# The gate matrix of an expert layer by accumulating scatters instead of one-hot matrix products

## The chip, the cores and the metric

One core of one Trainium2 chip runs the kernel. The metric is the time of one execution on the device in microseconds (us). Before the change it is 2658.03 us, the median of 3 runs (2650.47 to 2663.66).

## The reference

The reference is one encoder layer on two sequences, a long one of 512 tokens and a short one of 256: attention of two kinds, gates, projections, and then a layer of experts. All is in float32. The change concerns the experts:

```python
q = (t @ w_query).reshape(T, PEER_HEADS, 2, PEER_HALF)
s1 = jnp.einsum('thc,hkc->thk', q[:, :, 0], sub_keys_1)
s2 = jnp.einsum('thc,hkc->thk', q[:, :, 1], sub_keys_2)
v1, i1 = lax.top_k(s1, PEER_TOPK)
v2, i2 = lax.top_k(s2, PEER_TOPK)
cand = (v1[..., :, None] + v2[..., None, :]).reshape(T, PEER_HEADS, PEER_TOPK * PEER_TOPK)
top, ci = lax.top_k(cand, PEER_TOPK)
e1 = jnp.take_along_axis(i1, ci // PEER_TOPK, axis=-1)
e2 = jnp.take_along_axis(i2, ci % PEER_TOPK, axis=-1)
idx = (e1 * PEER_KEYS + e2).reshape(T, PEER_HEADS * PEER_TOPK)
g = jax.nn.softmax(top, axis=-1).reshape(T, PEER_HEADS * PEER_TOPK)
u = expert_u[idx]
a = jax.nn.gelu(jnp.einsum('ted,td->te', u, t), approximate=False)
out = jnp.einsum('te,ted->td', g * a, expert_v[idx])
```

Each token picks 16 of 16384 experts in each of 8 heads, 128 in all, each with a gate g. The tables expert_u and expert_v hold 16384 rows of 1024 numbers, 64 MB each.

## The kernel before, in words

The front (function front, first for the short sequence "p", then for the long one "s") does attention, projections and norms. It ends with w_query in four chunks of two heads; the scores of each chunk go through top16 on VectorE.

The experts are done in two ways. The short sequence gathers (gather, L814): for each of its two tiles of 128 tokens, 128 indirect DMAs fetch one row of u per token into a tile gr (512 KB, three buffers), VectorE multiplies and sums it (L828), and later 128 more fetch rows of v that VectorE adds up (L836). These 512 gathers are issued by GpSimd (L821) and are spread over everything that follows, by fill, which emits a step of the one generator for so much of the other.

The long sequence is dense: all 16384 experts are computed for all 512 tokens, and a matrix of gates, zero nearly everywhere, picks. It runs in blocks of 128 experts. A u block (stage1, L733) loads 512 KB, splits them into a high and a low part (split, L139: ScalarE rounds, VectorE subtracts) and makes 24 products of 128x512 (mm3, L144) into pu; ScalarE applies Gelu to it. 28 of the 128 results go to DRAM (ad), the others stay in SBUF. A v block (stage2 in dense, L757) multiplies a block's activations with its gates gt, splits the product and 128 rows of v, and makes 24 products into eight outputs of 128x512. Five of them (held) stay in PSUM; the other three are summed over groups of four blocks and then added on VectorE (L807), since the u blocks that run beside them need banks too.

The gate matrix is built in between. pick (L635), once for each tile of 128 tokens with its 8 heads, chooses the top 16 sums and their experts; the products pr of 1600 elements run on GpSimd (L675). gbuild (L705) then makes, for every token, two one-hot matrices (o1 on VectorE, o2 shared by GpSimd, ScalarE and VectorE by the table BY) and multiplies them on TensorE (L724) into a 128x128 matrix of gates, which ScalarE evicts and a DMA writes to gd:

```python
eng.tensor_scalar(o2, iota, sl[t][1][:, tk:tk + 1], sl[t][2][:, tk:tk + 1], op0=ALU.is_equal, op1=ALU.mult)
pe.matmul(p[:, j * 128:(j + 1) * 128], lhsT=o1[:, q % 8 + j, :], rhs=o2, start=True, stop=True)
```

The generators fix the order in which instructions are emitted, and a scheduler then orders each engine's queue by its own estimate of times. On the chip every engine and every DMA queue runs its list in order.

Of the kernel before, what the change touches and what calls it, by code (L numbers as in the profile page):

```python
# [11 lines left out]
F32 = mybir.dt.float32  # L12
# [15 lines left out]
GCH = 32  # L28
# [4 lines left out]
FILL = (2.25, 0.0, 3.7)  # L33
FG = 2.25
FL = {"p": 1, "s": 3}
BY = "aavvvvppavvvvppp"
B1, B2, B3 = 3, 8, 6
AT, SU, GP = (0.45, 0.25, 0.5)
UE = 3
# [5 lines left out]
ORDER, SLB = ('pppbpbbb', 3)  # L45
U0, UP, UB = (10, 0.25, 0.08)
# [3 lines left out]
def tile_peer(ctx: ExitStack, tc: tile.TileContext, a: dict):  # L50
# [23 lines left out]
    iota = cp.tile([128, 128], F32, name="iota")  # L74
# [7 lines left out]
    def consts():  # L82
        """rope tables with the gains of the first 16 dims, gain columns"""
# [19 lines left out]
        nc.sync.dma_start(iota, a["iota"])  # L103
# [11 lines left out]
    sl, slp = {}, []  # L115
# [6 lines left out]
    gd = dr.tile([S_S // GCH, 128, 128, GCH], F32, name="gd")  # L122

    anchor, banchor, turn, tog = [None], [None], [0], [0]
# [68 lines left out]
    def proj(pool, src, kts, Th, Tl, nt, name, onpool=0, unit=1.0):  # L193
        """per token tile PSUM [128, 512] of T^T @ src"""
# [10 lines left out]
    def proj_halves(last, src, Th, Tl, nt, name, onpool, done, unit):  # L205
        """proj of 8 row blocks, the first half of the token tiles before the second, done(t, acc) after each half"""
# [87 lines left out]
    def along(gen, other, rate=1.0):  # L294
        """gen with rate steps of other after each of its own, then what is left of other"""
# [35 lines left out]
    def front(seq):  # L331
# [6 lines left out]
        with ExitStack() as fs:  # L338
# [23 lines left out]
            with tc.tile_pool(name="att" + seq, bufs=1, reuse_waits="tile") as ap_:  # L362
# [12 lines left out]
                def post(c, raws):  # L375
                    """norm, rope and transposes of the query and key heads of chunk c"""
# [58 lines left out]
                # blocks: qa 0..3, qb0 4..5, kb0 6..7, qb1 qb2 8..11, kb1 kb2 12..15, ka 16  # L435
# [4 lines left out]
                def soft_pv(sm, n, negm, den, out, kvs):  # L440
                    """exp of -sm[:, :n] + negm, denominators, transposes, PV into out"""
# [62 lines left out]
                    # the dilated patterns stay within a tile of the order by class; the maximum goes on from the first pattern's  # L504
# [82 lines left out]
            vv = [pk.tile([128, 16, 16], F32, tag=f"vv{t}", name="vv") for t in range(nt)]  # L587
            iu = [pk.tile([128, 16, 16], U32, tag=f"iu{t}", name="iu") for t in range(nt)]
            for c in range(4):
                acc = [ps_mm(f"pq{m}", m // 2) for m in range(4)]  # L590
                # the first chunk of the long sequence takes the first half of its tokens before the second
# [12 lines left out]
                for m in range(4):  # L604
                    hh = 4 * c + m
# [7 lines left out]
                    for t in range(nt):  # L613
                        top16(pp, ss[:, t, :], 128, vv[t][:, hh, :], iu[t][:, hh, :])
# [12 lines left out]
    def gates(pool, w):  # L627
        """softmax over the 16 of a head, from the scores less their maximum"""
        ac.activation(w, w, AF.Exp)
        sm = pool.tile([128, 8], F32, tag="gsm", name="gsm", bufs=1)  # L630
        ve.tensor_reduce(sm, w, op=ALU.add, axis=AX.X)
        ve.reciprocal(sm, sm)
        ve.tensor_tensor(w, w, sm.unsqueeze(2).broadcast_to([128, 8, 16]), op=ALU.mult)

    def pick(pool, seq, t, vv, iu):  # L635
        """top 16 of the sums, their experts and gates"""
        fi = pool.tile([128, 8, 2, 16], F32, tag="fi", name="fi", bufs=1)
        ac.copy(fi.rearrange("p h z k -> p (h z) k"), iu)
        v4 = vv.rearrange("p (h z) k -> p h z k", z=2)
        cand = pool.tile([128, 8, NCAND], F32, tag="cand", name="cand", bufs=1)  # L640
        pos = 0
        for i, n in enumerate(CAND[:8]):
            ve.tensor_tensor(cand[:, :, pos:pos + n], v4[:, :, 1, 0:n], v4[:, :, 0, i:i + 1].broadcast_to([128, 8, n]), op=ALU.add)
            pos += n
        ve.tensor_tensor(cand[:, :, pos:pos + 8], v4[:, :, 0, 8:16], v4[:, :, 1, 0:1].broadcast_to([128, 8, 8]), op=ALU.add)
        tv = pool.tile([128, 8, 16], F32, tag="tv", name="tv", bufs=1)
        ti = pool.tile([128, 8, 16], U32, tag="ti", name="ti", bufs=1)
        # experts of all candidates, then those at the chosen positions
        ce = pool.tile([128, 8, NCAND], F32, tag="ce", name="ce", bufs=1)
        i1 = pool.tile([128, 8, 16], F32, tag="i1", name="i1", bufs=1)  # L650
        ac.mul(i1, fi[:, :, 0, :], 128.0)
        pos = 0
        for i, n in enumerate(CAND[:8]):
            gp.tensor_tensor(ce[:, :, pos:pos + n], fi[:, :, 1, 0:n], i1[:, :, i:i + 1].broadcast_to([128, 8, n]), op=ALU.add)
            pos += n
        gp.tensor_tensor(ce[:, :, pos:pos + 8], i1[:, :, 8:16], fi[:, :, 1, 0:1].broadcast_to([128, 8, 8]), op=ALU.add)
        yield 1
        for h in range(8):
# [3 lines left out]
        tf = pool.tile([128, 8, 16], BF16, tag="tf", name="tf", bufs=1)  # L662
        ve.tensor_copy(tf, ti)
        e = []
        for z in range(2):
            ez = pool.tile([128, 8, 16], F32, tag=f"e{z}", name=f"e{z}", bufs=1)
            e.append(ez)
        ex = pool.tile([128, 8, 16], F32, tag="ex", name="ex", bufs=1)
        yield 2
        for h in range(0, 8, 2):  # L670
            eq = pool.tile([128, 2, NCAND, 16], BF16, tag="eq", name="eq", bufs=2 if seq == "s" else 1)
            pr = pool.tile([128, 2, NCAND, 16], F32, tag="pr", name="pr", bufs=2 if seq == "s" else 1)
            ve.tensor_tensor(eq, posx.unsqueeze(1).broadcast_to([128, 2, NCAND, 16]),
                             tf[:, h:h + 2, :].unsqueeze(2).broadcast_to([128, 2, NCAND, 16]), op=ALU.is_equal)
            gp.tensor_tensor(pr, eq, ce[:, h:h + 2, :].unsqueeze(3).broadcast_to([128, 2, NCAND, 16]), op=ALU.mult)  # L675
            ve.tensor_reduce(ex[:, h:h + 2, :], pr.rearrange("p h c s -> p h s c"), op=ALU.add, axis=AX.X)  # L676
            yield 2
        if seq == "p":
            ve.tensor_tensor(pw[t].rearrange("p (h s) -> p h s", s=16), tv, tv[:, :, 0:1].broadcast_to([128, 8, 16]), op=ALU.subtract)
            ve.tensor_copy(pidx[t], ex.rearrange("p h s -> p (h s)"))  # L680
            yield 2
            return
        wt = pool.tile([128, 8, 16], F32, tag="wt", name="wt", bufs=1)
        ve.tensor_tensor(wt, tv, tv[:, :, 0:1].broadcast_to([128, 8, 16]), op=ALU.subtract)
        gates(pool, wt)
        ei = pool.tile([128, 128], I32, tag="ei", name="ei", bufs=1)
# [296 lines left out]
```

## Time and profile before

| what | value |
|---|---|
| median of 3 runs | 2658.03 us (2650.47 to 2663.66) |
| profiled execution, span | 2664.0 us; its slowest run is 2663.66 us, so the span is the whole time |
| TensorE, VectorE, ScalarE, GpSimd busy | 2416.8, 1955.7, 992.3, 1084.5 us |
| moved by DMA | 590.52 MB, 222 GB/s in the mean |
| gathers (queue of GpSimd) | 512, 268.47 MB |

Busy times are unions of an engine's instructions; products on TensorE overlap, so their mean length (0.39 us) is longer than their spacing. The clock that TensorE was granted is 0.96 of full speed in the mean.

### The profile page before, as it was taken

What the parts mean: (1) busy time and instruction counts of PE and PEld (TensorE: products, weight loads), DVE (VectorE), ACT (ScalarE), POOL (GpSimd) and SP (SyncE); (2) the same over time, 40 slices, a digit from 0 to 9 for tenths busy, and PEclk for the clock granted to TensorE, in tenths of its full rate; (3) what the DMA queues carried; (4) which work ended last, traced back from release to release, by engine and by line L of the source; (5) the groups of instructions that cost most, each with busy time, mean ns of one, the idle gap of its engine ahead of it and who ended that gap; (6) DMA issues with size and microseconds to landing.
All of it is one profiled execution on the core that took longest, in us unless ns stands there. A gap on an engine that the chain in (4) does not pass through costs nothing.

```text
span 2664.0 us, 33871 instructions
## 1 busy us (share of the span) xinstructions
PE 2416.8 (91%) x11926; PEld 1993.4 (75%) x11926; DVE 1955.7 (73%) x4018; ACT 992.3 (37%) x1656; POOL 1084.5 (41%) x808
## 2 busy tenths in 40 slices
PE   8999989999989988887999998988889999999998
PEld 6787867768768767776777876777777777777776
DVE  6755798677698899667477777676667677676776
ACT  5764434443433334879322221222122222222221
POOL 0001241454554165879232444444334444444342
PEclk9999989999989999999999999999999999999999
DMA  6425433576984232534889887788778788787776
GB/s 210 133 88 167 143 99 114 181 228 213 316 277 145 90 103 102 198 147 174 307 298 316 290 284 271 265 278 280 258 254 285 268 283 276 258 273 269 263 248 214
DMA packets 250058, 590.52 MB, mean 222 GB/s; under 512 B 19488, under 2 KB 107296, under 8 KB 247840
## 3 DMA queue, kind: packets, MB, share of 16 engines
q1 hardware_dynamic: 169824, 278.99, 32.0%
q0 software_dynamic: 73728, 268.47, 29.1%
q10 hardware_dynamic: 6336, 40.90, 3.8%
q8 instruction: 94, 1.54, 0.2%
q14 instruction: 76, 0.62, 0.1%
HBM read 535.57 MB, written 51.38 MB: 220 GB/s over the span
## 4 chain that ended last, share of the span: by engine, by line
DMA 30%; DVE 21%; PE 21%; issue 15%; POOL 10%; ACT 3%; SPq 1%; DVEq 0%; POOLq 0%; ACTq 0%
DMA gr<-v,pidx 13%; DMA gr<-u,pidx 7%; POOL o2g L723 5%; POOL gr L821 4%; DMA vr<-v 4%; DVE x L836 3%; DVE gr L828 2%; DVE ex L676 2%; DMA wraw<-w_in 2%; DVE ul L141 2%; DVE vl L141 2%; DMA gl<-ad 2%; DVE wlo L141 1%; PE p_g L724 1%; PE pu L147 1%
## 5 line engine op out<-in xcount | busy, mean ns | idle before, releaser
L821 POOL DMA_INDIRECT gr<-v,pidx x256 | 346.7, 1354 | 490.6 <-DVE x L836 293.6
L821 POOL DMA_INDIRECT gr<-u,pidx x256 | 315.9, 1234 | 519.6 <-DVE gr L828 243.6
L836 DVE SCALAR_TENSOR_TENSOR x<-gr,act,x 128x1024 f32<-128x1024 f32 x256 | 328.5, 1283 | 208.7 <-DMA gr<-v,pidx 206.6
L828 DVE SCALAR_TENSOR_TENSOR gr<-gr,tok 128x1024 f32<-128x1024 f32 x256 | 337.4, 1327 | 180.6 <-DMA gr<-u,pidx 179.7
L145 PE MATMUL pu<-tTh,uh 128*128 128x512 f32 x1024 | 405.5, 396 | 26.3 <-ACT ga__15105 L745 5.9
L147 PE MATMUL pu<-tTh,ul 128*128 128x512 f32 x1024 | 406.5, 397 | 25.0 <-DVE ul L141 24.9
L146 PE MATMUL pu<-tTl,uh 128*128 128x512 f32 x1024 | 403.4, 394 | 0.0
L141 POOL TENSOR_TENSOR wlo<-wraw,whi 128x1024 fp32r<-128x1024 f32 x51 | 124.2, 2435 | 372.9 <-ACT whi L140 350.8
L140 ACT CAST uh<-ur 128x1024 fp32r<-128x1024 f32 x128 | 134.6, 1052 | 327.8 <-PE pu L146 238.0
L147 PEld LDWEIGHTS pu<-tTh,ul 128*128 128x128 f32 x1024 | 195.5, 191 | 71.1 <-DVE ul L141 30.6
L145 PEld LDWEIGHTS pu<-tTh,uh 128*128 128x128 f32 x1024 | 195.7, 191 | 69.8 <-ACT ga__15105 L745 6.4
L146 PE MATMUL held<-vl,ph 128*128 128x512 f32 x640 | 242.0, 392 | 0.0
L147 PE MATMUL held<-vh,pl 128*128 128x512 f32 x640 | 241.0, 390 | 0.0
L145 PE MATMUL held<-vh,ph 128*128 128x512 f32 x640 | 240.6, 396 | 0.0
L140 ACT CAST vh<-vr 128x1024 fp32r<-128x1024 f32 x128 | 134.3, 1049 | 278.4 <-DMA vr<-v 269.5
L145 PE MATMUL py<-vh,ph 128*128 128x512 f32 x384 | 166.2, 433 | 77.0 <-DVE y L807 63.2
L146 PEld LDWEIGHTS pu<-tTl,uh 128*128 128x128 f32 x1024 | 195.1, 190 | 40.7
L723 POOL TENSOR_SCALAR o2g<-iota,sl,sl 128x128 f32<-128x128 f32 x160 | 198.8, 1254 | 36.7 <-PE p_g L724 36.7
L140 ACT CAST whi<-wraw 128x1024 fp32r<-128x1024 f32 x137 | 143.7, 1049 | 159.7 <-DMA wraw<-w_in 53.7
L141 DVE TENSOR_TENSOR ul<-ur,uh 128x1024 fp32r<-128x1024 f32 x128 | 172.0, 1344 | 36.0 <-ACT uh L140 36.0
L141 DVE TENSOR_TENSOR vl<-vr,vh 128x1024 fp32r<-128x1024 f32 x128 | 156.4, 1222 | 21.4 <-ACT vh L140 21.2
L145 PEld LDWEIGHTS py<-vh,ph 128*128 128x128 f32 x384 | 78.3, 204 | 110.5 <-DVE y L807 77.2
(710 smaller groups left out, 5345.1 us busy)
## 6 DMA issues: line engine op xcount, KB each, us to landing
ur<-ublk SPq DMA_DIRECT2D x128, 512.0 KB, 4.7
vr<-v SPq DMA_DIRECT2D x128, 512.0 KB, 6.3
wraw<-w_in SPq DMA_DIRECT2D x80, 512.0 KB, 3.6
gd<-gs ACTq DMA_DIRECT2D x16, 2048.0 KB, 6.7
gt<-gd SPq DMA_DIRECT2D x32, 1024.0 KB, 10.1
wraw<-w_query SPq DMA_DIRECT2D x32, 512.0 KB, 3.8
wraw<-w_out SPq DMA_DIRECT2D x16, 512.0 KB, 4.1
gl<-ad SPq DMA_DIRECT2D x28, 256.0 KB, 7.1
```

What stands on the lines that cost most here:

```text
L140: i = ac.copy(hi, src)
L141: eng.tensor_tensor(lo, src, hi.bitcast(F32), op=ALU.subtract)
L145: pe.matmul(out, lhsT=lh, rhs=rh, start=first, stop=False)
L146: pe.matmul(out, lhsT=lh, rhs=rl, start=False, stop=False)
L147: pe.matmul(out, lhsT=ll, rhs=rh, start=False, stop=last)
L676: ve.tensor_reduce(ex[:, h:h + 2, :], pr.rearrange("p h c s -> p h s c"), op=ALU.add, axis=AX.X)
L723: eng.tensor_scalar(o2, iota, sl[t][1][:, tk:tk + 1], sl[t][2][:, tk:tk + 1], op0=ALU.is_equal, op1=ALU.mult)
L724: pe.matmul(p[:, j * 128:(j + 1) * 128], lhsT=o1[:, q % 8 + j, :], rhs=o2, start=True, stop=True)
L821: st = gp.indirect_dma_start(out=g, out_offset=None, in_=tab, in_offset=bass.IndirectOffsetOnAxis(ap=pidx[t][:, s:s + 1], axis=0))
L828: ve.scalar_tensor_tensor(g, g, 1.0, tok, op0=ALU.mult, op1=ALU.mult, accum_out=act[:, s:s + 1])
L836: ve.scalar_tensor_tensor(xt, g, act[:, s:s + 1], xt, op0=ALU.mult, op1=ALU.add)
```

## The change

Instead of one-hot matrices, the gates are added into a gate matrix in DRAM that was zeroed before (clear, in the front, by GpSimd's queue). For each of the four tiles t of 128 tokens there is one matrix gd[t]. A pick now covers one chunk of two heads for all tiles, so it has 32 experts per tile and token; scatter issues, for each of these 32 and each tile, one indirect DMA that adds 128 numbers (one per token) at 128 addresses. The products pr and the sums ce of pick move from GpSimd to VectorE. All u blocks come before the first v block, their activations all go through DRAM, and the v blocks then have all eight banks of PSUM. In this last part gathers have five more row buffers (gr2). The diff, cut to its core:

```diff
+U0, UP, US, GU = (8, 0.45, 0.16, 0.11)
+GV = 2.2
+GR2 = 5
-    gd = dr.tile([S_S // GCH, 128, 128, GCH], F32, name="gd")
+    gd = [dr.tile([128 * 128 * 128, 1], F32, name=f"gd{t}") for t in range(4)]
...
-            gp.tensor_tensor(pr, eq, ce[:, h:h + 2, :].unsqueeze(3).broadcast_to([128, 2, NCAND, 16]), op=ALU.mult)
-            ve.tensor_reduce(ex[:, h:h + 2, :], pr.rearrange("p h c s -> p h s c"), op=ALU.add, axis=AX.X)
+            ve.tensor_tensor(pr, eq.rearrange("p h c s -> p h s c"), ce[:, h:h + 2, :].unsqueeze(2).broadcast_to([128, 2, 16, NCAND]), op=ALU.mult)
+            ve.tensor_reduce(ex[:, h:h + 2, :], pr, op=ALU.add, axis=AX.X)
...
+        ve.tensor_scalar(si, ex.rearrange("p h s -> p (h s)"), 128.0, pcol, op0=ALU.mult, op1=ALU.add)
+        slots[c] = (si, wt.rearrange("p h s -> p (h s)"))
...
+    def scatter(c):
+        si, wt = slots[c]
+        for s in range(32):
+            for t in range(4):
+                k = t * 32 + s
+                gp.indirect_dma_start(out=gd[t], out_offset=bass.IndirectOffsetOnAxis(ap=si[:, k:k + 1], axis=0),
+                                      in_=wt[:, k:k + 1], in_offset=None, compute_op=ALU.add)
+            yield 1
+    def clear():
+        z = gpl.tile([128, D], F32, tag="gr", name="zero", bufs=3)
+        gp.memset(z, 0.0)
+        for t in range(4):
+            v = gd[t].rearrange("(p q k d) o -> q p k (d o)", p=128, q=4, d=D)
+            for q in range(4):
+                st = gp.dma_start(v[q], z.unsqueeze(1).broadcast_to([128, 4, D]))
...
-        if j < SP:
-            nc.scalar.dma_start(ad[j], ga)
-        else:
-            acts[j] = ga
+        nc.scalar.dma_start(ad[j], ga)
...
-        held = [psd.tile([128, 512], F32, name=f"held{i}") for i in range(5)]
+        held = [psd.tile([128, 512], F32, name=f"held{i}") for i in range(8)]
...
-                if own or g == ng - 1:
-                    ve.tensor_tensor(x[t][:, cs], py, x[t][:, cs], op=ALU.add)
+                mm3(held[i], ph[:, c], pl[:, c], vh[:, cs], vl[:, cs], j == 0, j == 127)
+                if j == 127:
+                    ve.tensor_tensor(x[t][:, cs], held[i], x[t][:, cs], op=ALU.add)
...
+            more = len(gp2) and s % (GR2 + 3) >= 3
+            g = (gp2[0] if more else pool).tile([128, D], F32, tag="gr2" if more else "gr", name="gr", bufs=GR2 if more else 3)
...
+    for c in range(4):
+        fill(pick(pks["s"][1], "s", c, *tops["s"][c]), ua, UP, due)
+    for c in range(4):
+        for _ in scatter(c):
+            due[0] += US * 4
+            gdue[0] += GU * 4
...
+    fill(dense(pv_, psd), gg, GV)
```

How the queues change is seen at three places. On GpSimd, the rows from the last products of the picks on stood like this (o2g is a one-hot matrix; a name in brackets is what the instruction waits for, DMASW being DMAs that GpSimd issued):

```order
L675 TENSOR_TENSOR pr<-eq,ce 128x1600 [waits DVE_49,Pool_49]
L675 TENSOR_TENSOR pr<-eq,ce 128x1600 [waits DVE_49]
L675 TENSOR_TENSOR pr<-eq,ce 128x1600 [waits DVE_49,Pool_49] x2
L723 TENSOR_SCALAR o2g<-iota,sl_9613,sl_9614 128x128 [waits PE_49] x27
L723 TENSOR_SCALAR o2g<-iota,sl_9910,sl_9911 128x128 [waits PE_49,Activation_49]
L723 TENSOR_SCALAR o2g<-iota,sl_9910,sl_9911 128x128 [waits PE_49] x39
```

and now, behind the last split of weights (gd_91 to gd_94 are the four matrices):

```order
L138 TENSOR_TENSOR wlo<-wraw,whi 128x1024 [waits DMAHW6_49,PE_49,Activation_49]
L696 DMA gd_91<-wt,si 2097152x1 [waits DMASW0_49,DVE_49]
L696 DMA gd_92<-wt,si 2097152x1 [waits DMASW1_49]
L696 DMA gd_93<-wt,si 2097152x1 [waits DMASW2_49]
L696 DMA gd_94<-wt,si 2097152x1 [waits DMASW3_49]
L696 DMA gd_91<-wt,si 2097152x1 [waits DMASW4_49,DMASW0_49]
L696 DMA gd_92<-wt,si 2097152x1 [waits DMASW5_49,DMASW1_49]
L696 DMA gd_93<-wt,si 2097152x1 [waits DMASW6_49,DMASW2_49]
L696 DMA gd_94<-wt,si 2097152x1 [waits DMASW7_49,DMASW3_49]
L696 DMA gd_91<-wt,si 2097152x1 [waits DMASW4_49]
```

In all, 512 scatters follow, 202 of them without a gather between, then 310 with 50 gathers; 104 gathers stand before them and 358 behind.

On SyncE, at the change from u to v blocks, the changed kernel has (ur is a u block, gt the gates, vr rows of v, gl activations):

```order
L716 DMA ur<-ublk 128x1024 [waits DMAHW6_49,DVE_49]
L737 DMA gt<-gd_91 128x512 [waits DMAHW5_49,DMASW6_49,DMASW0_49]
L737 DMA gt<-gd_92 128x512 [waits DMASW7_49,DMASW4_49]
L737 DMA gt<-gd_93 128x512 [waits DMAHW7_49,DMASW3_49,DMASW0_49]
L737 DMA gt<-gd_94 128x512 [waits DMAHW1_49,DMASW1_49]
L716 DMA ur<-ublk 128x1024 [waits DMAHW2_49,DMAHW0_49,DVE_49]
L739 DMA vr<-v 128x1024 [waits DMAHW3_49]
L741 DMA gl<-ad 128x512 [waits DMAHW4_49,PE_49]
```

The loads of gt wait for scatters, and some of the u loads stand behind them.

On VectorE at the same place (ul is the split of a u block, x adds up gathered rows of v):

```order
L138 TENSOR_TENSOR ul<-ur,uh 128x1024 x2
L797 SCALAR_TENSOR_TENSOR x_80<-gr,act,x_80 128x1024
L746 TENSOR_TENSOR gl<-gl,gt 128x512
L138 TENSOR_TENSOR vl<-vr,vh 128x1024
L138 TENSOR_TENSOR ul<-ur,uh 128x1024
L746 TENSOR_TENSOR gl<-gl,gt 128x512
L138 TENSOR_TENSOR pl<-gl,ph 128x512
```

The first product with gt stands behind 112 splits ul; the other 16 stand behind it.

## Rows read from the trace of the kernel before

**Rows 1.** The page, part 1 (busy time of each engine) and part 4 (chain).

```profile
PE 2416.8 (91%) x11926; PEld 1993.4 (75%) x11926; DVE 1955.7 (73%) x4018; ACT 992.3 (37%) x1656; POOL 1084.5 (41%) x808
...
DMA 30%; DVE 21%; PE 21%; issue 15%; POOL 10%; ACT 3%; SPq 1%; DVEq 0%; POOLq 0%; ACTq 0%
```

**Rows 2.** Windows by stage: length, each engine's busy time, TensorE clock, DMA share, GB/s.

```profile
0.00:897.00 897.00, 825.75 (x4749) 692.28 (x4750) 674.14 (x2061) 401.95 (x782) 279.72 (x190) 0.96 0.53 173
897.00:973.00 76.00, 65.10 (x274) 52.01 (x273) 75.81 (x293) 24.49 (x39) 26.88 (x24) 0.96 0.34 118
973.00:1281.00 308.00, 254.13 (x1529) 218.00 (x1528) 233.86 (x527) 219.94 (x388) 236.23 (x188) 0.97 0.39 151
1281.00:1462.00 181.00, 170.53 (x707) 137.59 (x708) 123.68 (x164) 52.02 (x64) 45.70 (x37) 0.95 0.93 318
1462.00:2587.00 1125.00, 1037.18 (x4392) 841.75 (x4391) 797.17 (x923) 280.79 (x370) 472.20 (x351) 0.97 0.80 271
```

**Rows 3.** Groups by line: busy us, mean ns, idle before and its releaser.

```profile
L145 PE MATMUL py<-vh,ph 128*128 128x512 f32 x384 | 166.2, 433 | 77.0 <-DVE y L807 63.2 <-ACT ph L140 8.3 <-ACT vh L140 4.7
L725 ACT COPY gs<-p_g 128x512 f32<-128x512 f32 x128 | 132.8, 1086 | 2.6 <-PE p_g L724 2.3
L724 PE MATMUL p_g<-o,o 128*128 128x128 f32 x512 | 72.1, 279 | 3.5 <-DVE o L723 3.2
L807 DVE TENSOR_TENSOR y<-py,y 128x512 f32<-128x512 f32 x96 | 64.7, 685 | 4.3 <-PE py L147 4.3
```

**Rows 4.** Waits, whole span: us in total, times, longest us.

```profile
POOL gr L821 <- DVE x L836: 296.9, 145, 7.0
...
DVE x L836 <- DMA gr<-v,pidx: 206.6, 110, 5.7
```

**Rows 5.** Timeline of TensorE in a u block: start us, duration us.

```profile
1290.21 0.39 PE L146 MATMUL pu<-tTl,uh 128*128 128x512 f32 x1
1290.43 0.39 PE L147 MATMUL pu<-tTh,ul 128*128 128x512 f32 x1
```

**Rows 6.** Timeline of GpSimd, two gathers without a wait for a buffer.

```profile
799.85 0.94 POOL L821 DMA_INDIRECT gr<-u,pidx  x1 [0.30 <-issue]
801.10 0.94 POOL L821 DMA_INDIRECT gr<-u,pidx  x1 [0.30 <-DVE tTl L141]
```

**Rows 7.** Tile gr (ns min/median/max, first and last start) and page part 5 (busy us, mean ns).

```profile
L821 POOL DMA_INDIRECT gr<-u,pidx x256: 932/995/1987, 445.3 to 2231.5; - x128
L821 POOL DMA_INDIRECT gr<-v,pidx x256: 932/1146/4797, 1399.4 to 2647.4; - x128
...
L821 POOL DMA_INDIRECT gr<-v,pidx x256 | 346.7, 1354 | 490.6 <-DVE x L836 293.6
L821 POOL DMA_INDIRECT gr<-u,pidx x256 | 315.9, 1234 | 519.6 <-DVE gr L828 243.6
```

**Rows 8.** Timelines: VectorE's first top-16, GpSimd's last split, ScalarE behind the last top-16.

```profile
821.96 0.67 DVE L620 MAX8 vv<-ss 128x8 f32<-128x128 f32 x3
...
877.28 2.40 POOL L141 TENSOR_TENSOR wlo<-wraw,whi 128x1024 fp32r<-128x1024 f32 x1 [8.05 <-ACT whi L140]
...
915.77 0.41 ACT L638 CAST fi<-iu 128x256 f32<-128x256 uint32 x1 [0.68 <-DVE iu L624]
```

**Rows 9.** Groups of VectorE by line: busy us, mean ns.

```profile
L836 DVE SCALAR_TENSOR_TENSOR x<-gr,act,x 128x1024 f32<-128x1024 f32 x256 | 328.5, 1283 | 208.7 <-DMA gr<-v,pidx 206.6
L141 DVE TENSOR_TENSOR vl<-vr,vh 128x1024 fp32r<-128x1024 f32 x128 | 156.4, 1222 | 21.4 <-ACT vh L140 21.2
L676 DVE TENSOR_REDUCE ex<-pr 128x32 f32<-128x1600 f32 x24 | 70.2, 2926 | 0.0
L768 DVE TENSOR_TENSOR gl<-gl,gt 128x512 f32<-128x512 f32 x28 | 19.3, 689 | 11.8 <-DMA gl<-ad 11.8
```

**Rows 10.** DMA issues: KB each, median us from issue to landing.

```profile
gr<-u,pidx POOLq DMA_INDIRECT x256, 5.9
...
ad<-ga__9081 ACTq DMA_DIRECT2D x1, 256.0 KB, 2.0
```

More of the change, by code (lines that the diff above doesn't have):

```diff
@@ L641, in pick @@
+    def pick(pool, seq, c, vv, iu):
+        nt = 4 if seq == "s" else 2
+        n2 = 2 * nt
+        fi = pool.tile([128, n2, 2, 16], F32, tag="fi", name="fi", bufs=1)
+        ac.copy(fi.rearrange("p h z k -> p (h z) k"), iu.rearrange("p t m k -> p (t m) k"))
+        v4 = vv.rearrange("p t (h z) k -> p (t h) z k", z=2)
+        cand = pool.tile([128, n2, NCAND], F32, tag="cand", name="cand", bufs=1)
         pos = 0
         for i, n in enumerate(CAND[:8]):
[L643 removed]
+            ve.tensor_tensor(cand[:, :, pos:pos + n], v4[:, :, 1, 0:n], v4[:, :, 0, i:i + 1].broadcast_to([128, n2, n]), op=ALU.add)
@@ L644, in pick @@
             pos += n
[L645 to L650, printed above, removed]
+        ve.tensor_tensor(cand[:, :, pos:pos + 8], v4[:, :, 0, 8:16], v4[:, :, 1, 0:1].broadcast_to([128, n2, 8]), op=ALU.add)
@@ L661, in pick @@
                 yield 1
-        tf = pool.tile([128, 8, 16], BF16, tag="tf", name="tf", bufs=1)
+        tf = pool.tile([128, n2, 16], BF16, tag="tf", name="tf", bufs=1)
         ve.tensor_copy(tf, ti)
[L664 to L672, printed above, removed]
+        ex = pool.tile([128, n2, 16], F32, tag="ex", name="ex", bufs=1)
@@ L673, in pick @@
+        for h in range(0, n2, 2):
+            eq = pool.tile([128, 2, NCAND, 16], BF16, tag="eq", name="eq", bufs=1)
+            pr = pool.tile([128, 2, 16, NCAND], F32, tag="pr", name="pr", bufs=1)
             ve.tensor_tensor(eq, posx.unsqueeze(1).broadcast_to([128, 2, NCAND, 16]),
                              tf[:, h:h + 2, :].unsqueeze(2).broadcast_to([128, 2, NCAND, 16]), op=ALU.is_equal)
-            gp.tensor_tensor(pr, eq, ce[:, h:h + 2, :].unsqueeze(3).broadcast_to([128, 2, NCAND, 16]), op=ALU.mult)
@@ L680, in pick @@
-            ve.tensor_copy(pidx[t], ex.rearrange("p h s -> p (h s)"))
+            for t in range(nt):
+                k = slice(32 * c, 32 * c + 32)
+                h = slice(2 * t, 2 * t + 2)
+                ve.tensor_tensor(pw[t][:, k].rearrange("p (h s) -> p h s", s=16), tv[:, h, :], tv[:, h, 0:1].broadcast_to([128, 2, 16]), op=ALU.subtract)
+                ve.tensor_copy(pidx[t][:, k], ex[:, h, :].rearrange("p h s -> p (h s)"))
             yield 2
             return
-        wt = pool.tile([128, 8, 16], F32, tag="wt", name="wt", bufs=1)
@@ new lines, in stage2 @@
+                for t in range(4):
+                    nc.sync.dma_start(gts[g][:, t], gd[t].rearrange("(p e t) o -> p e (t o)", e=128, t=128)[:, g * GRP:(g + 1) * GRP, :])
+            vr = pv_.tile([128, D], F32, tag="vr", name="vr", bufs=3)
+            nc.sync.dma_start(vr, vrows[j])
+            ga = pv_.tile([128, S_S], F32, tag="gl", name="gl", bufs=3)
+            nc.sync.dma_start(ga, ad[j])
+            vh = pv_.tile([128, D], F32R, tag="vh", name="vh", bufs=3)
+            vl = pv_.tile([128, D], F32R, tag="vl", name="vl", bufs=3)
@@ L798, in dense @@
+        nxt = stage2(0)
+        for j in range(128):
+            ph, pl, vh, vl = nxt
+            if j < 127:
+                nxt = stage2(j + 1)
+            if j >= 120 and j < 124:
+                t = j - 120
+                x[t] = pv_.tile([128, D], F32, name=f"y{t}")
+                nc.sync.dma_start(x[t], xs[t * 128:(t + 1) * 128, :])
+            for i in range(8):
                 t, n = divmod(i, 2)
@@ L866, in tile_peer @@
     gpl = ctx.enter_context(tc.tile_pool(name="ga", bufs=1, side="right", reuse_waits="tile"))
-    run(front("p"))
+    zero = clear()
+    fill(front("p"), zero, 0.5)
+    run(zero)
     def picks_p():
-        for t in range(2):
-            yield from pick(pks["p"][1], "p", t, *tops["p"][t])
+        for c in range(4):
+            yield from pick(pks["p"][1], "p", c, *tops["p"][c])
         pks["p"][0].__exit__(None, None, None)
@@ L879, in ahead @@
     def ahead():
-        for j in range(SP + LA):
+        for j in range(128):
             stage1(j, pu_, ps, ("mm", "mb"))
@@ L886, in tile_peer @@
         next(ua)
-    with tc.tile_pool(name="gb", bufs=1, side="right", reuse_waits="tile") as gpool:
-        slp.append(gpool)
-        P = [pick(pks["s"][1], "s", t, *tops["s"][t]) for t in range(4)]
-        B = [gbuild(gpool, t) for t in range(4)]
-        due = [0.0]
-        most = islice(ua, SP + LA - U0 - UE)
-        it = {"p": iter(P), "b": iter(B)}
-        for k in ORDER:
-            g = next(it[k])
-            fill(weave(g, gg, FILL[1]) if k == "b" else g, most, UP if k == "p" else UB, due)
-        run(most)
-        run(ua)
-        banchor[0] = None
+    due, gdue = [0.0], [0.0]
+    for c in range(4):
+        fill(pick(pks["s"][1], "s", c, *tops["s"][c]), ua, UP, due)
+    for c in range(4):
+        for _ in scatter(c):
+            due[0] += US * 4
+            gdue[0] += GU * 4
+            while due[0] >= 1.0:
+                due[0] -= 1.0
+                next(ua, None)
+            while gdue[0] >= 1.0:
+                gdue[0] -= 1.0
+                next(gg, None)
+    run(ua)
     pks["s"][0].__exit__(None, None, None)
     psx[0].__exit__(None, None, None)
+    gp2.append(ctx.enter_context(tc.tile_pool(name="gr2", bufs=1, side="right", reuse_waits="tile")))
     psd = ctx.enter_context(tc.tile_pool(name="psd", bufs=1, space=PSUM))
     pv_ = ctx.enter_context(tc.tile_pool(name="dv", bufs=1, reuse_waits="tile"))
-    fill(dense(pu_, pv_, psd), gg, FILL[2])
+    fill(dense(pv_, psd), gg, GV)
     run(gg)
```

168 lines of the change are left out of this document (42 added, 126 removed).

## The prediction

> **What bounds the kernel now.** I read the page first: TensorE is busy for 91% of the span, yet the chain that ended last is 30% DMA, 21% VectorE and only 21% TensorE [rows 1]. A mean like that hides stages with different limits, so I cut the span at the marks of the program [rows 2]. Up to 897 us runs the front (attention and projections). From 897 to 1281 us the experts of the long sequence are picked and the gate matrix is built, with 36 of the 128 u blocks in between. After 1281 us come the other 92 u blocks, all 128 v blocks and 406 of the 512 gathers.
>
> In the gate stage the DMA engines idle (share 0.34 and 0.39) and ScalarE, GpSimd, VectorE and TensorE share the work of the one-hot matrices [rows 2, 3]. In the last stage it is the other way: right after 1281 us the DMA engines are at a share of 0.93 and 318 GB/s, later at 0.80 and 271 GB/s [rows 2]. The later fall is a wait: VectorE waits for gathered rows and GpSimd waits for VectorE to free one of three row buffers [rows 4].
>
> TensorE alone would need less. Its products of 512 columns follow each other every 0.227 us [rows 5], so a u or v block of 24 products takes 5.44 us, and all 256 take 1393 us.
>
> **What the change removes.** Between 897 and 1281 us lie 384 us with 36 u blocks, which need 36 x 5.44 = 196 us; the gate matrix thus costs about 188 us now. The 1024 one-hot products, their operand builders and the 128 evictions go [rows 3]. So do the 96 additions of partial sums, for which TensorE stood 63 us [rows 3]: eight outputs stay in PSUM, and the order of the changed kernel has eight final additions instead. On TensorE the change is a clear gain; what counts is what takes its place.
>
> **What it adds on GpSimd.** 512 scatters stand in one row on GpSimd, in the order's first piece, with 50 gathers between the later ones. Each adds 128 numbers, one per partition, into one of four matrices, and waits for the previous scatter into the same matrix, that is the fourth before it. No scatter is in the trace. The nearest row is the gather of 128 rows by a list of indices, the same form of instruction: at its fastest 0.94 us with a gap of 0.30 us before it when nothing holds it up [rows 6], median 0.995 us early and 1.146 us later, at most 4.8 us [rows 7]. Moving fewer bytes could make it cheaper, reading its destination could make it dearer; neither is shown. I take the median of the first kind and the gap, 0.995 + 0.30 = **1.30 us**, because it comes from stages in which VectorE is less loaded. The ends are 0.9 us (the fastest issue with no gap) and 1.98 us (below, rival 3).
>
> That median has VectorE as a neighbour: gathers last 0.93 us at least and 1.23 to 1.35 us in the mean [rows 7], so something stretches them. The Trainium skill, "SBUF — State Buffer", section "Who interferes with whom", says that GpSimd shares a pair of SBUF ports with VectorE, and that a DMA issued from GpSimd stalls when its descriptor generation is starved of that port. By that rule the scatters would take the later gathers' mean; the trace agrees in so far as the durations spread, and cannot say why. That version is rival 2.
>
> When can the first scatter run? Picks now go by chunk of heads, so the first pick needs only the first chunk's scores. VectorE begins the top-16 work on these at 822 us [rows 8] and is through just before 916 us [rows 8]. In the new order 150 of its 320 instructions stand before the first index list: 93 x 150/320 = 44 us. The pick itself is 40 instructions of top-16 on 50 candidates (under 0.29 us each, which is 93/320: 10 us), 18 small additions and four comparisons (some 8 us, an estimate from 0.69 us for 512 elements [rows 9]), four reductions of 2.93 us at most and four products of 1600 elements, moved from GpSimd to VectorE, at 1222 ns x 1600/1024 = 1.9 us [rows 9]: 38 us. That makes 822 + 44 + 38 = 904 us; GpSimd's last weight split, at 880 us [rows 8], is in time. The clearing of the matrix is 16 stores of 2 MB, 33.5 MB in the front, where the DMA share is 0.53 [rows 2]. I cost it at 5 us, because loads of weights there are hidden by TensorE work; its bound is 33.5 MB at 318 GB/s, 105 us, if all of it stood in the way. First scatter: **909 us**.
>
> The scatters end at 909 + 512 x 1.30 + 50 x 1.25 = 909 + 666 + 63 = **1638 us**. Beside them TensorE runs u blocks: the other three picks (3 x 38 us), the rest of the scores' top-16 (49 us) and 24 u blocks (24 x 1.22 us) hold VectorE until 904 + 192 = 1096 us, and the next 87 u blocks take 473 us, to 1569 us. There it stops, as the order's third piece shows: VectorE's next instruction multiplies with the gate matrix, and 16 u blocks stand behind it; on SyncE the loads of the gate matrix wait for the last scatters with the remaining u loads behind them (second piece). So the scatters set the end of this stage, and TensorE stands about 70 us. The longer picks on VectorE cost nothing as long as this is so. Those of the short sequence (eight products of 1.9 us, 15 us) lie in the front, where VectorE is busy for 674 of 897 us [rows 2]; I cost them at nothing, 15 us if that slack is elsewhere.
>
> **What lies after the last scatter.** By the order: 16 u blocks, 128 v blocks, 358 gathers (279 between the first gate product and the first final addition, 78 behind it). In DMA bytes, with 0.524 MB for a 512 KB tile: 358 gathers 187.7 MB; v rows 67.1, activations read back 33.5 (all 128 blocks now go through DRAM, before only 28), gate matrix 33.5, u blocks and their stores 12.6, residual and output 4.2. Sum 338.7 MB. TensorE needs 144 x 5.44 = 783 us for it, VectorE 128 x (1.22 + 2 x 0.69) + 358 x 1.30 + 16 x 1.22 = 818 us [rows 9]. The DMA engines need more: at 318 GB/s, the best that the trace holds over 181 us [rows 2], 338.7/0.318 = **1065 us**. I take that rate because the change gives the gathers eight buffers instead of three, which removes the wait of [rows 4]. Its bounds are 318/0.93 = 342 GB/s (990 us) and 271 GB/s (1250 us, if the buffers don't help). The last 78 gathers run with TensorE idle, but in a stage that DMA bounds this costs nothing more. The end (last product, last store) is 8 us.
>
> Sum: 1638 + 1065 + 8 = 2711 us against the profiled 2664, that is +47 us. The profiled execution lies 6 us above the median of the runs, so I forecast **2704 us**, 1.7% more than 2658. The sum shows where it turns: with the rest as it is, the kernel is even at (2664 - 909 - 63 - 1073)/512 = 1.21 us for a scatter, just under the fastest gather with its gap, 1.24 us. A difference under 0.5% is about what a measurement of this kernel can't tell from none.
>
> **Rivals.**
> 1. Faster. Scatters at 1.24 us or less and DMA near its full share: 909 + 635 + 63 + 990 + 8 = 2605 us. If a scatter takes under (1569 - 909 - 63)/512 = 1.17 us, TensorE sets the end of the u stage (1569 us), and the floor is 1569 + 990 + 8 = 2567 us. For it speaks that undisturbed gathers do keep 0.94 + 0.30 us [rows 6] and that a share of 0.93 was reached with three buffers [rows 2]; against it that the median is longer [rows 7]. It decides below 1.21 us for a scatter, or above 334 GB/s with 1.30 us (1638 + 1014 + 8 = 2660). Chance 0.35.
> 2. Scatters stretched like the gathers of the last stage: 1.354 + 0.30 = 1.65 us [rows 6, 7], end 909 + 845 + 63 + 1073 = 2890 us. Against it: VectorE is less loaded here. Chance 0.13.
> 3. The wait takes over. Four matrices are four chains; a scatter can't be issued before the fourth before it has landed. Gathers land 5.9 us after their issue and stores of 256 KB 2.0 us [rows 10]. If a scatter needs both, one after the other, a chain turns in 7.9 us and a scatter takes 7.9/4 = 1.98 us: 909 + 1014 + 63 + 1073 = 3059 us. With 5.9 us alone it is 1.48 us and 2803 us. It decides from 5.2 us of landing on (4 x 1.30). For it speaks that nothing on GpSimd can overtake a waiting scatter; against it that small transfers land in about 2 us [rows 10]. The Trainium skill, "DMA: Bandwidth & Descriptors", section "Rules for kernel authors", says that an accumulating DMA reads its destination and writes it later, with nothing holding the bytes in between, so that another accumulation on them has to wait for the first one's semaphore; that is why the chains can't be dropped. No run here shows an accumulating DMA yet. Chance 0.12.
>
> That the change doesn't do what it says is ruled out: the order holds 512 scatters, no one-hot product and eight final additions.
>
> **How the numbers follow.** The forecast's own case (1.24 to 1.5 us for a scatter, 1030 to 1090 us behind) has 0.40 and spans 2645 to 2790 us; about 0.08 of it is no change. Faster has rival 1's 0.35; slower the rest of the forecast's case and rivals 2 and 3, 0.32 + 0.13 + 0.12 = 0.57. The range of 8 in 10 runs from 2550 us (rival 1 down to its floor) to 2930 us (rival 2 and the mild form of rival 3); outside stay the hard form of rival 3 and what none of these cases holds.
>
> **What would show it.** Right: the scatters' spacing on GpSimd at 1.24 to 1.5 us; the first at about 909 us, the last at about 1640 us; TensorE nearly idle just before; behind it a DMA share over 0.9 at about 318 GB/s and no long waits of VectorE for gathers. Wrong: a spacing under 1.2 us with TensorE dense in the u stage; scatters that wait for landings (idle time before them put down to DMA); or a last stage as slow as 271 GB/s in spite of the eight buffers, which would add 185 us.

## The result, and the profile after

The changed kernel takes **2971.71 us** (median of 4 runs, 2967.27 to 2979.78) against 2654.25 us of the kernel before on the same chip: a ratio of 1.1187 (95% interval 1.1155 to 1.1218). It is slower by 12%, where 1.7% was forecast, and 42 us above the upper end of the range. In the sessions of the experiments below the kernel before took 2667 to 2669 us, so a difference from the changed kernel's profiled 2968 us is uncertain by some 12 us there; most experiments are a single execution.

The page of the changed kernel, parts 1, 2 and 4 (busy times; the span in 40 slices; the chain), beside [rows 1]:

```profile
PE 2334.2 (79%) x10890; PEld 1907.7 (64%) x10890; DVE 1792.2 (60%) x3717; ACT 814.0 (27%) x1315; POOL 1633.8 (55%) x1099
...
PE   6899869999987999103666667767999999999950
...
POOL 0000200555554888888888888886045445544456
...
GB/s 253 284 259 174 161 68 105 206 219 269 283 200 61 121 124 154 18 0 68 115 133 114 127 122 124 116 126 220 222 293 404 402 403 403 394 402 395 397 368 359
...
PE 32%; POOL 26%; DVE 16%; DMA 14%; issue 10%; ACT 2%; SPq 0%; ACTq 0%; POOLq 0%; DVEq 0%
```

GpSimd is now the second largest part of the chain, behind TensorE (26%, before 10%). In the middle of the span it is busy for eight tenths of every slice, and the DMA engines move mostly some 120 GB/s; in a hole of TensorE, which falls to 0 there, they move 0 to 68 GB/s. After that some 400 GB/s flow; no slice of the kernel before is above 316. The stages show it; the columns are those of [rows 2], and the cuts are the first scatter, a hole of TensorE, the last scatter and the last product:

```profile
0.00:946.00 946.00, 830.39 (x4660) 693.47 (x4661) 695.15 (x2072) 394.35 (x775) 272.44 (x180) 0.94 0.60 198
946.00:1190.00 244.00, 227.29 (x993) 184.41 (x992) 182.35 (x604) 76.80 (x103) 211.99 (x106) 0.99 0.58 127
1190.00:1390.00 200.00, 21.14 (x82) 16.59 (x81) 3.51 (x4) 6.17 (x8) 167.08 (x109) 0.56 0.27 15
1390.00:2049.00 659.00, 456.27 (x1662) 355.33 (x1663) 142.84 (x144) 106.68 (x139) 552.82 (x349) 0.86 0.58 123
2049.00:2880.00 831.00, 799.09 (x3497) 657.89 (x3496) 686.22 (x832) 229.96 (x291) 370.87 (x301) 0.99 0.97 371
2880.00:2968.00 88.00, 0.00 (x0) 0.00 (x0) 82.12 (x64) 0.00 (x0) 58.58 (x58) 0.50 0.93 365
```

The scatters themselves, from the view of their line (durations min/median/max in ns, first and last start; then what ended GpSimd's idle time before them) and from the groups by line (busy us, mean ns):

```profile
L696 POOL DMA_INDIRECT gd<-wt,si x512: 1546/1554/6200, 945.9 to 2046.9; - x171
...
  issue: 151.8, 498
  DMA gd<-wt,si: 4.0, 13
...
DMA to landing us min/median/max: 2.9/3.2/7.7
```

```profile
L696 POOL DMA_INDIRECT gd<-wt,si x512 | 881.9, 1722 | 157.1 <-issue 151.8 <-DMA gd<-wt,si 4.0 <-DVE vv L620 1.3
```

A scatter never takes less than 1.546 us, with 0.30 us between two; the gather that I priced it by takes 0.995 us in the median and 0.94 at its fastest [rows 6, 7]. Waits for an earlier scatter to land sum to 4.0 us. What TensorE and VectorE wait for most:

```profile
PE pu L144 <- DVE ul L138: 386.3, 63, 177.8
```

```profile
DVE gr L789 <- DMA gr<-u,pidx: 489.1, 65, 184.6
```

In the hole, a gather stands in GpSimd's queue behind the first 202 scatters (it starts at 1368.8 us), VectorE stands at the product of its row, the low part of the next u block stands behind that in VectorE's queue, and TensorE waits for the low part.

### The profile page after: what moved, and what is told of

Its sections match the earlier page's. It is cut to its first block, busy times and chain, and to the rows that moved or that the text cites. A ratio compares the mean times of both kernels' runs of the same rounds, so it can differ in the third digit from the quotient of the medians.

```text
span 2968.1 us, 31969 instructions
## 1 busy us (share of the span) xinstructions
PE 2334.2 (79%) x10890; PEld 1907.7 (64%) x10890; DVE 1792.2 (60%) x3717; ACT 814.0 (27%) x1315; POOL 1633.8 (55%) x1099
## 4 chain that ended last, share of the span: by engine, by line
PE 32%; POOL 26%; DVE 16%; DMA 14%; issue 10%; ACT 2%; SPq 0%; ACTq 0%; POOLq 0%; DVEq 0%
POOL gd L696 23%; PE held L142 5%; PE held L143 5%; PE held L144 5%; DMA vr<-v 4%; DVE x L797 3%; DMA gr<-u,pidx 2%; DMA wraw<-w_in 2%; POOL gr L782 2%; PE pu L144 2%; DVE gr L789 2%; PE pu L142 2%; PE pu L143 2%; DMA gl<-ad 2%; DMA gd<-wt,si 1%
## 5 line engine op out<-in xcount | busy, mean ns | idle before, releaser
L696 POOL DMA_INDIRECT gd<-wt,si x512 | 881.9, 1722 | 157.1 <-issue 151.8
L144 PE MATMUL pu<-tTh,ul 128*128 128x512 f32 x1024 | 437.6, 428 | 386.5 <-DVE ul L138 386.3
L782 POOL DMA_INDIRECT gr<-v,pidx x256 | 297.1, 1161 | 321.3 <-ACT ph L137 214.8
L143 PE MATMUL held<-vl,ph 128*128 128x512 f32 x1024 | 398.4, 389 | 0.0
L144 PE MATMUL held<-vh,pl 128*128 128x512 f32 x1024 | 398.3, 389 | 0.0
L142 PE MATMUL held<-vh,ph 128*128 128x512 f32 x1024 | 278.4, 390 | 3.4 <-ACT vh L137 2.7
L142 PEld LDWEIGHTS held<-vh,ph 128*128 128x128 f32 x1024 | 192.0, 188 | 44.7 <-ACT vh L137 3.9
L144 PEld LDWEIGHTS held<-vh,pl 128*128 128x128 f32 x1024 | 192.3, 188 | 39.9
L143 PEld LDWEIGHTS held<-vl,ph 128*128 128x128 f32 x1024 | 192.2, 188 | 39.9
L137 ACT CAST ph<-gl 128x512 fp32r<-128x512 f32 x128 | 79.6, 622 | 472.3 <-DVE gl L746 402.9
```

Source lines behind the costliest of these rows:

```text
L137: i = ac.copy(hi, src)
L142: pe.matmul(out, lhsT=lh, rhs=rh, start=first, stop=False)
L143: pe.matmul(out, lhsT=lh, rhs=rl, start=False, stop=False)
L144: pe.matmul(out, lhsT=ll, rhs=rh, start=False, stop=last)
L696: gp.indirect_dma_start(out=gd[t], out_offset=bass.IndirectOffsetOnAxis(ap=si[:, k:k + 1], axis=0), in_=wt[:, k:k + 1], in_offset=None, co ...
L782: st = gp.indirect_dma_start(out=g, out_offset=None, in_=tab, in_offset=bass.IndirectOffsetOnAxis(ap=pidx[t][:, s:s + 1], axis=0))
```

## The experiments

**1. Scatters that don't add.** The edit:

```diff
-                                      in_=wt[:, k:k + 1], in_offset=None, compute_op=ALU.add)
+                                      in_=wt[:, k:k + 1], in_offset=None)
```

> The changed kernel with scatters that write their gate instead of adding it (compute_op left out). It leaves out the sum where two heads of a token pick the same expert: the later gate replaces the earlier. In the changed kernel a scatter is 1.55 us on GpSimd with 0.30 us before it, where an undisturbed gather of 128 whole rows is 0.94 us. Theory A, the addition is what a scatter costs more than a gather: the median falls to 0.94 to 1.0 us, 512 x 0.58 = 297 us go, and the time is about 2670 us. Theory B, the price is that of writing 128 single numbers at listed places, whether added or not: the median stays at 1.55 us and the time within 10 us of 2968.

The one run took 2807.23 us. A scatter now lasts as long as a gather, but its profile has a stretch from about 955 to 1122 us in which VectorE starts an instruction only every 1.4 us, for no reason that the profile shows. So the same kernel ran again:

> The kernel with scatters that write instead of adding, a second time, for one thing in its first profile: between about 955 and 1122 us VectorE began an instruction only every 1.4 us, each waiting for nothing that the profile shows, while a scatter stood on GpSimd every 1.28 us; TensorE stood. Theory A, that belongs to this kernel (scatters close to each other hold VectorE up, where the longer scatters of the changed kernel don't): the stretch is there again, and the time is within 15 us of 2807. Theory B, it was that one execution: VectorE is busy there as in the changed kernel, and the time is about 2650 to 2720 us.

```profile
L696 POOL DMA_INDIRECT gd<-wt,si x512: 965/970/5503, 960.1 to 1780.4; - x171
```

2702.66 and 2701.92 us, without that stretch: it was that one execution, its cause stays open, and the 2702 us are used from here. Theory A holds: the addition makes a scatter 1.554 instead of 0.970 us, and costs 2968 - 2701 = 267 us of span. Against the kernel before, the ratio of the kernel that only writes is 1.012 (1.0067 to 1.0173).

**2. Half as many numbers in a scatter** (`si[0:64, ...]` and `wt[0:64, ...]` in the same call).

> The changed kernel with scatters of 64 numbers instead of 128. It leaves out the gates of the second 64 tokens of each tile. Theory A, a scatter is priced by its numbers (8 ns of issue for each with the addition): 1.55 us falls to about 0.8 us, the scatters end some 390 us earlier, at about 1660 us, and the time is about 2580 us. Theory B, it is priced by the instruction: 1.55 us stays and the time is within 15 us of 2968. Between them, a fixed part and a part per number, the median says which.

```profile
L696 POOL DMA_INDIRECT gd<-wt,si x512: 1412/1421/5682, 950.0 to 1988.9; - x171
```

2925.40 us. (Theory A's 8 ns would leave 1.55 - 64 x 0.008 = 1.04 us and not its 0.8.) Half the numbers save 0.133 us of 1.554, so between 64 and 128 a number costs 2 ns, and on a straight line through these two points 1.29 us are left for the instruction: nearer to theory B. Shorter instructions gain little; that fewer, each with more numbers, would gain more is not shown, as no run measured one. The page's part 3 says what GpSimd's DMA queue moved (packets, MB, share), here for the changed kernel, then for plain scatters, half scatters and none:

```profile
q0 software_dynamic: 155904, 302.32, 35.4%
```

```profile
q0 software_dynamic: 98560, 302.32, 30.9%
```

```profile
q0 software_dynamic: 123136, 302.19, 33.1%
```

```profile
q0 software_dynamic: 82176, 302.02, 32.6%
```

Less the last and divided by 512, an adding scatter of 128 numbers makes 144 packets, one of 64 makes 80, and a plain one of 128 makes 32. The counts are 16 more than the numbers added, as if every added number travelled in a packet of its own. At 2 ns each, an estimate, the 112 packets more would be 0.23 of the 0.58 us that the addition costs; where the rest arises in GpSimd stays open.

**3. No scatters at all** (the call replaced by `pass`).

> The changed kernel without its 512 scatters; picks, clearing and all else stay, so the gate matrix is zero and the experts of the long sequence give nothing. Theory A, the scatters alone set the end of the u stage (946 to 2049 us): without them TensorE does, the first u block starts at about 966 us, 128 blocks of 5.44 us end at about 1662 us instead of 2158, and the stage behind keeps its 919 us counted from the first gate product: about 2470 us (2440 to 2540, as gathers move). Theory B, the order of the queues holds the u stage as well (TensorE stands 386 us for low parts of u, VectorE 489 us for gathers): a good part of these waits stays without the scatters, and the time is above 2650 us.

2494.78 us, with 2666.56 us for the kernel before beside it. From the first gate product on (u blocks, v blocks, tail):

```profile
1117.00:1680.00 563.00, 560.34 (x2466) 462.18 (x2465) 206.26 (x200) 163.44 (x213) 75.86 (x60) 1.00 0.63 214
1680.00:2380.00 700.00, 696.90 (x3066) 574.48 (x3065) 621.89 (x771) 199.91 (x252) 343.78 (x277) 1.00 1.01 388
2380.00:2493.00 113.00, 4.34 (x20) 3.26 (x18) 104.92 (x86) 0.00 (x0) 73.22 (x71) 0.54 0.94 363
```

TensorE is dense from the first u block to 2380 us, and the holes are gone. Theory A holds: in this order of the queues the scatters cost 2968 - 2493 = 475 us, and all the rest of the change gains 2667 - 2495 = 172 us.

**4. No gathers between the scatters** (`GU` from 0.11 to 0.0).

> The changed kernel with the 50 gathers that stood between the scatters moved behind them. VectorE then has no gather to wait for before the last scatter, so TensorE's 386 us of waiting for low parts of u go from the middle of the u stage. Theory A, the scatters set the end of the stage and these waits cost nothing: the scatters end 50 x 1.3 = 65 us earlier (about 1985 us), all u blocks are done by then, 50 gathers more lie behind (26 MB, 68 us at 385 GB/s), 16 u blocks less (33 us): 2900 to 2970 us. Theory B, the waits of TensorE in the u stage cost their own time: 2968 - 386 = about 2580 us, in any case below 2800 us.

2996.42 us: no faster. The hole in the middle goes, another takes its place, as SyncE's and TensorE's waits show:

```profile
SPq L737 <- DMA gd<-wt,si: 433.8, 3, 430.4
```

```profile
PE pu L142 <- ACT uh L137: 433.7, 2, 428.9
```

Now TensorE gets far ahead, and then SyncE holds the loads of the last u blocks back behind a load of the gate matrix, until the last scatter (1945.4 us). The direction is theory A's: TensorE's waits in this stage move with the order, and taking the 386 us out of the middle buys nothing while the scatters last. The time is 26 us above the top of its band. The band had counted on all u blocks being done by the last scatter, but some 26 were still held then; they end at 2111 us.

**5. One chain instead of four**: each scatter also waits for the one before.

```diff
+                if last:
+                    tc.add_manual_dep(st.ins, last[0].ins.name, SYNC, reason="pace")
+                last[:] = [st]
```

> The changed kernel with every scatter waiting for the one before it, whatever its matrix: one chain instead of four. Theory A, a scatter can be followed only when it has landed, 3.2 us after its issue by the changed kernel's profile: scatters follow each other every 3.3 to 3.6 us (5.1 us if the 3.2 us count from the end of the 1.55 us), the stage grows by 512 x 1.4 to 3.0 us = 700 to 1500 us, and the time is 3650 to 4500 us; four chains turn in 4 x 1.86 = 7.4 us and so hide it. Theory B, the four chains were of no use, as GpSimd's own time covers the landing: within 20 us of 2968.

```profile
L696 POOL DMA_INDIRECT gd<-wt,si x512: 1544/1552/5429, 946.7 to 2885.0; - x171
...
  DMA gd<-wt,si: 999.6, 510
```

3717.42 us. Without the 50 gathers, a scatter every (2885.0 - 946.7 - 65)/511 = 3.7 us. The wait for a landing is real and dear, 1000 us in all; four chains hide it (13 waits, 4.0 us). That is the accumulation rule of the Trainium skill, "DMA: Bandwidth & Descriptors", section "Rules for kernel authors", with its price: an addition must wait for the earlier one on the same bytes, and the order of the loops (matrix inside, expert outside) keeps that wait off the path. What is lost without the wait no run here shows.

**6. The low parts of u not on VectorE** (`ac.copy(ul, ur)` on ScalarE).

> The changed kernel with the low part of each u block made by a second cast on ScalarE instead of a subtraction on VectorE (it leaves the subtraction out, so the low part is the whole number again). In the changed kernel 512 scatters last 1.722 us in the mean and 1.554 in the median; what they last over 1.554 sums to 87 us, about 44 us of it in scatters beside a subtraction of the u blocks and most of the rest beside the picks' products of 1600 elements. Theory A, VectorE's instructions with two inputs stretch the scatters that run beside them: without the subtractions about 44 us of the 87 go, and the last scatter comes that much earlier. Theory B, the long scatters have another cause (the DMA engines, the rows of the gathers): the sum stays at 80 us or more.

```profile
L696 POOL DMA_INDIRECT gd<-wt,si x512 | 848.9, 1658 | 158.2 <-issue 154.6 <-DVE vv L620 2.4 <-DMA gd<-wt,si 1.2
```

2935.83 us; what the scatters last over 1.554 us falls from 881.9 - 512 x 1.554 = 86 us to 53 us, a little less than theory A said. The timeline of the changed kernel says why, if one asks which VectorE instruction is running when a scatter starts. For 109 scatters it is one that reads two operands from SBUF; 108 of these are stretched, and they hold 84 of the 86 us. For 33 it is one that reads one operand (maxima, index searches, sums), and 370 start beside none; four of all these 403 are longer by more than 0.03 us, and together they hold 2 us. Of the 84 us, 31 stand beside subtractions of u blocks, which fits the 33 that go without them; 27 stand beside products and sums of gathered rows, which the expectation's 44 had in part put down to the subtractions, and 27 beside the picks (rounded). One beside a product of 1600 elements, GpSimd's row first, then VectorE's:

```profile
985.72 4.26 POOL L696 DMA_INDIRECT gd<-wt,si  x1 [0.30 <-issue]
```

```profile
985.34 3.26 DVE L669 TENSOR_TENSOR pr<-eq,ce 128x1600 f32<-128x1600 bf16 x1
```

And two beside the product of a gathered row with its token:

```profile
1400.19 1.56 POOL L696 DMA_INDIRECT gd<-wt,si  x1 [0.30 <-issue]
```

```profile
1401.15 1.23 DVE L789 SCALAR_TENSOR_TENSOR gr<-gr,tok 128x1024 f32<-128x1024 f32 x1 [6.60 <-DMA gr<-u,pidx]
```

```profile
1402.05 1.75 POOL L696 DMA_INDIRECT gd<-wt,si  x1 [0.30 <-issue]
```

The scatter that was under way when the product began keeps 1.56 us. The one that starts during it ends 1.42 us after the product's end; beside the products and sums of gathered rows the median is 1.43 us. So a scatter that starts beside such an instruction makes hardly any progress until that is over. The Trainium skill, "SBUF — State Buffer", section "Who interferes with whom", has two operands contend with a GpSimd instruction that reads SBUF, and the rows agree. It also infers that descriptor generation escapes that; these scatters, which read their indices from SBUF and generate descriptors, don't escape, and which of the two is held no run here tells apart.

**7. Three row buffers in the last stage** instead of eight (`more = False`).

> The changed kernel with three row buffers for the gathers in the last stage as before, instead of eight. The last stage moves 385 to 400 GB/s with eight, and moved 271 to 318 GB/s in the kernel before. Theory A, the buffers made the rate: with three it falls back to about 295 GB/s, and the 338.7 MB behind the last scatter take 1148 us instead of 919: about 3200 us. Theory B, the rate comes with the order (all v blocks together, eight outputs kept in PSUM, no u blocks beside them), not with the buffers: within 30 us of 2968.

```profile
2032.00:2820.00 788.00, 779.27 (x3423) 642.64 (x3422) 577.04 (x707) 226.69 (x290) 261.32 (x208) 1.00 0.90 327
2820.00:3176.00 356.00, 15.63 (x69) 12.59 (x68) 200.87 (x189) 1.04 (x2) 156.45 (x151) 0.53 0.72 231
```

3178.19 us, so the buffers are worth 206 us, close to what theory A said. TensorE runs as dense as with eight (779 of 788 us); it is the gathers that fall back, and the tail without TensorE grows from 88 to 356 us.

**8. No clearing, no scatters**; the gates are read from the table of v.

> The changed kernel without scatters and without clearing; the gates are read from the table of v instead (numbers without meaning), so that nothing is read that wasn't written. To be compared with the kernel without scatters alone (2493 us, first u block at 963 us). Theory A, the 33.5 MB of zeros hold the front up: the first u block comes 40 to 60 us earlier (at 905 to 925 us, in the kernel before the front ends at 897 us). Theory B, the zeros are hidden and the longer front has another cause (the picks of the short sequence now wholly on VectorE): the first u block within 10 us of 963 us.

2492.32 us. When the four index lists are written, without and with clearing (both without scatters):

```profile
L684 DVE TENSOR_SCALAR si<-ex,pcol x4: 269/282/301, 908.4 to 1073.8; 128x128 int32<-128x128 f32 x4
```

```profile
L684 DVE TENSOR_SCALAR si<-ex,pcol x4: 268/278/301, 942.7 to 1107.0; 128x128 int32<-128x128 f32 x4
```

Clearing holds the front up by 34 us; the first u block starts at 929 instead of 963 us, a little less of a gain than theory A's 40 to 60. Without scatters this buys nothing at the end (2492 against 2495 us).

**9. The order of the changed kernel with the old gate build.** Picks and one-hot matrices as before, then all u blocks, then v with eight outputs in PSUM, and the five further buffers from the end of the gate build on. From the kernel before:

```diff
+    gp2.append(ctx.enter_context(tc.tile_pool(name="gr2", bufs=1, side="right", reuse_waits="tile")))
+    fill(ua, gg, GU)
...
+    fill(dense(pv_, psd), gg, GV)
```

with GU = 2.2, GV = 1.55, dense from the changed kernel, its gate loads from the kernel before, and all activations through DRAM.

> The other half of the change alone: the gate matrix built with one-hot matrices as before, but then all u blocks first, v blocks behind them with eight outputs in PSUM, all activations through DRAM, and the five further row buffers (here from the end of the gate build on). Without scatters that half gave 2493 us, 171 us less than the kernel before. Theory A, the gain of that half holds under the old gate build as well: the gate stage ends at 1281 us with 36 u blocks done, TensorE then needs 92 + 128 blocks of 5.44 us = 1197 us, and about 421 MB at 385 GB/s (1094 us) fit beside it: about 2490 us. Theory B, VectorE is the bound there (92 x 1.22 + 128 x 2.6 + 406 x 1.30 = 973 us busy, in an order in which it waits for rows): 1300 us or more for this stage, 2580 us or more.

```profile
897.00:1281.00 384.00, 318.61 (x1805) 270.07 (x1803) 310.37 (x821) 246.34 (x426) 262.94 (x212) 0.97 0.40 150
1281.00:1826.00 545.00, 528.93 (x2297) 434.13 (x2298) 373.72 (x387) 158.79 (x196) 244.57 (x206) 0.98 0.97 356
1826.00:2529.00 703.00, 698.72 (x3078) 577.20 (x3076) 550.29 (x659) 198.28 (x252) 272.49 (x201) 1.00 0.96 335
```

**2535.09 us**, a ratio of 0.9525 (0.9478 to 0.9572) to the kernel before: faster than both. TensorE is busy for 1228 of the last 1248 us, so theory A holds. Its 2490 us counted 36 u blocks before 1281 us; 32 fit (1805 products less 1024 one-hot ones and 12 transposes, by 24), and four more cost 22 of the 45 us missing. The time lies half way between the two theories' numbers; what decides for A is that TensorE, and not VectorE, is busy throughout.

## Why the prediction was wrong, point by point

- **The price of a scatter: this step failed.** "The nearest row is the gather of 128 rows by a list of indices, the same form of instruction", hence 1.30 us. The form decides only for a scatter that writes: 0.970 + 0.30 us undisturbed (experiment 1). The addition, which no row of before showed, raises it to 1.554 + 0.30. On 512 scatters that is 512 x 0.554 = 284 us, and 86 us of stretching by VectorE come on top (experiment 6). The stage from the first scatter to the last took 1103 us where the sum had 729. My upper end for it, 1.98 us, came from a wait for landings and not from the instruction; the mean, (1103 - 65)/512 = 2.03 us, lies above even that. That the kernel that only writes takes 2702 us, next to the forecast 2704, is luck: its first scatter comes 51 us later than forecast, its scatters are stretched by 93 us (590.0 - 512 x 0.970 us busy), and the last stage is 154 us shorter.
- **The first scatter**: forecast 909 us, measured 945.9. The term mis-sized is the clearing, 34 us and not 5 (experiment 8). Without it the first index list comes at 908.4 us, where the sum had 904: the top-16 work on the first chunk's scores begins at 831.6 us instead of 822, and the picks take 77 us instead of 82, so these two errors half cancel.
- **"The scatters set the end of this stage"**: right. But TensorE stood 386 us for low parts of u rather than 70 at the stage's end; the longest of these waits, 178 us, lies in its middle. The sum let 24 and then 87 u blocks run beside the scatters (by the order it is 112, one more) and had nothing for a gathered row that VectorE waits for while its gather stands behind 202 scatters. Longer scatters made that wait longer, but it is there without them: the kernel that only writes waits 150 us for low parts of u, as the row below shows. No run shows a price of this wait alone: without scatters nothing holds the stage (experiment 3), and with the gathers moved behind them the time is no shorter (experiment 4).

```profile
L144 PE MATMUL pu<-tTh,ul 128*128 128x512 f32 x1024 | 421.4, 412 | 150.7 <-DVE ul L138 150.3
```

- **The last stage**: forecast 1073 us with the end, measured 919. The step "1065 us at 318 GB/s" was mis-sized: 338.7 MB moved at 369 GB/s in the mean, up to 404. Nor was 342 GB/s a ceiling: the share of 0.93 from which I scaled it belonged to another mix of transfers, and at 0.97 to 1.01 the changed order moved 371 to 388 GB/s. That the buffers remove the wait of [rows 4] was right; they are worth 206 us (experiment 7).
- **The sum**: 2711 + 37 for the first scatter + 374 for the stage - 154 behind it = 2968 us, the measured span.
- **Rival 1** had its condition for the DMA met and that for the scatter missed by far; its break-even of 1.21 us stands to measured 1.85 undisturbed. **Rival 2**'s mechanism is there, with 86 us instead of 512 x 0.35 = 179. **Rival 3** did not happen: a landing takes 3.2 us from its issue, and four chains turn in 4 x 1.85 = 7.4 us; with one chain it does happen (experiment 5).

The whole comes to this: the change consists of a gain of 172 us (order, PSUM, buffers, no one-hot work) and of scatters that cost 475 us, of which the addition is 267. The difference, 303 us, falls short of the measured 317 by about what the kernel before varied between sessions.

## What to carry to other kernels

The trace may show an instruction's form without its operation: here an indirect DMA, but none that adds. The nearest row then doesn't price it, and an upper bound has to allow for the operation itself. If 512 of them stand in one queue, one run with a few of them is worth more than any sum. Where a change joins several edits, cost and try each alone: here the part that gives the change its name loses 475 us, and the new order with the old gate build beats the two kernels by 5% and 15%. Row buffers for gathers can set the DMA rate of a whole stage; here eight instead of three gave 206 us.

## What the runs showed of the hardware that I had not expected

- An indirect DMA of 128 single numbers occupies GpSimd for 0.97 us if it writes them and 1.55 us if it adds them; of the latter some 1.29 us don't depend on how many there are, if 64 and 128 (1.42 and 1.55 us) lie on a straight line.
- An adding scatter makes far more packets (144 for 128 numbers, 32 when written), yet it lands nearly as fast: 3.2 us after its issue against 2.8 us.
- A scatter that starts while VectorE runs an instruction with two operands from SBUF ends some 1.43 us after that instruction; one that has already started isn't stretched (experiment 6).
- In one of three executions of the kernel that writes, VectorE started one instruction every 1.4 us for some 165 us beside dense scatters, and the time was 2807 instead of 2702 us. Nothing in the profile says why.
